# An encoder's tiles moved by 384 bytes: the weights' parts at the operands' place modulo 512

## The chip, the cores and the metric

The kernel runs on one core of a Trainium2 chip. The metric is the device time of one execution in microseconds (us); the time before is the median of three runs. The chip is told of only as this case's runs and traces show it.

## The reference

Two layers over 256 tokens of width 2048, all in float32; each layer reads its 262 MB of weights once.

```python
for i in range(DEPTH):                      # DEPTH = 2
    h = rmsnorm(x, g_mix[i])
    z = h @ w_in[i]                         # diff q, k, v | latents | rope key | two gates
    ...                                     # 8 heads of differential attention -> od
    y_diff = od.reshape(b, s, DIFF_WIDTH) @ w_branch_diff[i]
    ...                                     # 8 heads of multi-head latent attention -> om
    y_mla = om.reshape(b, s, MLA_WIDTH) @ w_branch_mla[i]
    merged = jax.nn.sigmoid(ga) * y_diff + jax.nn.sigmoid(gb) * y_mla
    x = x + merged @ w_out[i]
    gu = rmsnorm(x, g_ffn[i]) @ w_gate_up[i]
    gate, up = jnp.split(gu, 2, axis=-1)
    x = x + (jax.nn.silu(gate) * up) @ w_down[i]
    e = p[i] @ w_ple_in[i]
    x = x + jax.nn.sigmoid(rmsnorm(x, g_ple[i]) @ w_ple_gate[i]) * e
return rmsnorm(x, g_final)
```

## The kernel before

Activations are held with the channels on the 128 partitions and the 256 tokens along the free dimension. Every float32 operand of a large product is split into a high part (rounded to the matmul's fp32r type) and a low part (the rest). An operand of a product, `ua[j]` or `ub[j]`, is one tile of 512 columns: 256 of the high part, then 256 of the low part.

`piece` (line 167) fetches up to eight 128x128 blocks of a weight in one transfer of up to 512 KB, issued on the SyncE queue, into one of four buffers `w32`; ScalarE writes the high part `whi` (line 176), VectorE the low part `wlo` (through the helper on line 72); both have three buffers. `emit` (line 196) then issues a pair of matmuls for each block: line 206 holds the block of `whi` as weights and streams all 512 columns of the operand; line 207 holds the block of `wlo` and streams the operand's first 256 columns. Each matmul is preceded by the load of its own 128x128 weights, 512 bytes of each partition. In the profile a matmul stands under PE and its weight load under PEld, with the line of the matmul. A product over 2048 channels is 16 such pairs. ScalarE and VectorE afterwards join the two halves of the result (lines 231 and 72).

The scores of the second attention (line 336, tiles `S<-fb,fa` and `S<-kr,fc` or `S<-kr,ub`) are blocks of twelve matmuls of 256 columns, each with its own weight load; those that apply the probabilities to the values (line 615, `at<-wt,E`) are blocks of six. The first value product (lines 387 to 389, `mmv<-whi,ua`) streams the weights, 512 columns at a time, and holds the operand.

The order on each engine is set when the program is built, by a scheduler with a timeline of its own; the transfers of the weights are issued ahead as far as the four buffers go.

Tiles that live through the whole kernel stand in the order in which they are made. In the built program `ua` and `ub` come first, at a distance of 2048 bytes, and all begin at 128 modulo 512 (bytes within a partition); then `xT`, at 128; then `gcol`, the factors of the norms, 126 columns (504 bytes, which take up 512); then `rc` and the rest, among them the 128x128 tiles `ident` and `ones` and the slots `fa0` to `fa4` at 160, `kr`, `fb`, `fc` and `fa5` to `fa7` at 256. The temporary pools follow. There `w32`, `whi`, `wlo`, `E`, `E1` and `wt` begin at 256. A weight block is 512 bytes wide and an operand's part 1024, so that every block of `whi` and `wlo` begins at 256 and every part of `ua` and `ub` at 128.

Of the kernel before, what the change touches and what calls it, by code (L numbers as in the profile page):

```python
# [12 lines left out]
F32 = mybir.dt.float32  # L13
# [6 lines left out]
P = 128  # L20
# [16 lines left out]
PT = 8  # L37
W_BUFS = 4
WARM = 8
NO_SYNC = mybir.DependencyInfo(mybir.DependencyClass.NoSync, mybir.DependencyReason.DATA)  # L40

TWO_PI = 2.0 * math.pi
# [8 lines left out]
def encoder(ctx, tc, x, p, positions, cols, lams, wq, wk, wv, wcq, wckv, wkr, wga, wgb,  # L51
# [5 lines left out]
    const = pool("const")  # L57
# [10 lines left out]
    def bank(ps=ps_at, tag="at", name="at", shape=(P, 2 * T)):  # L68
        return ps.tile(list(shape), F32, tag=tag, name=name)
# [22 lines left out]


    xT = const.tile([P, NC, T], F32, name="xT")
    gcol = const.tile([P, cols.shape[1]], F32, name="gcol")
    rc = const.tile([P, rope_c.shape[1]], F32, name="rc")
    nc.scalar.dma_start(gcol, cols)
    off = {}
# [301 lines left out]
    warm = bank()  # L400
    for _ in range(WARM):
        PE.matmul(warm[:, :P], ones, ones, start=True, stop=True)
# [8 lines left out]
    for L in range(DEPTH):  # L411
# [120 lines left out]
        def sigmoid(sg):  # L532
            si = A.activation(sg, sg, AF.Sigmoid)
            tc.add_manual_dep(si.ins, last_exp[0].ins.name, NO_SYNC, reason="one change of tables")

# [248 lines left out]
```

## Time and profile before

| | us |
|---|---|
| median of three runs (2933.39 to 2934.36) | 2933.75 |
| the profiled execution's own time | 2934.72 |
| its span in the trace | 2932.9 |
| PE busy | 2914.7 |
| PEld (weight loads) busy | 2550.8 |
| DVE busy | 2063.6 |
| ACT busy | 1524.5 |

The profiled execution is 0.97 us longer than the median, and its span 1.8 us shorter than its own time. A busy PE says that some matmul was under way at every moment, not that the array took a column at every clock: matmuls overlap, and their ends are modelled. How fast a stage goes is therefore read from the starts of successive matmuls, or from their number in a window of time.

### The profile page before, as it was taken

The page shows a single profiled execution, that of the slowest core. Times are in us where ns is not written, and L with a number is a line of the kernel's source. Part 1 is how long each engine was busy: PE and PEld are TensorE (multiplying, and loading weights), DVE is VectorE, ACT ScalarE, POOL GpSimd, SP SyncE. Part 2 cuts the span into 40 slices and gives each one's busy share as a digit, 9 for nine tenths or more (in the row PEclk, how much of TensorE's full clock was granted, in tenths as well). Part 3 has the DMA queues.
Part 4 walks back from the last instruction along what each step waited for, and adds up shares of the span by engine and source line. Part 5 has one row for each costly group of instructions (what it writes and reads, how often), then busy time and mean ns, then how long its engine had stood idle before and what let it go on. Part 6 is the DMA issues. An engine that isn't in the chain of part 4 may idle for free.

```text
span 2932.9 us, 43979 instructions
## 1 busy us (share of the span) xinstructions
PE 2914.7 (99%) x16750; PEld 2550.8 (87%) x16750; DVE 2063.6 (70%) x3529; ACT 1524.5 (52%) x2529; POOL 1.6 (0%) x8
## 2 busy tenths in 40 slices
PE   9999999999999999999999999999999999999998
PEld 7888888888888888888888888888888888888887
DVE  7897658776666666666859975687666666666676
ACT  6676545544444444445646755455444444444454
POOL 0000000000000000000000000000000000000000
PEclk9999999999999999999999999999999999999999
DMA  6444455555565565555554444555555655655654
GB/s 229 166 161 148 158 188 191 187 186 187 183 193 188 178 191 195 187 187 186 187 186 165 150 153 164 189 190 186 187 187 182 192 188 181 194 188 188 188 185 140
DMA packets 156019, 532.40 MB, mean 182 GB/s; under 512 B 16928, under 2 KB 23840, under 8 KB 155808
## 3 DMA queue, kind: packets, MB, share of 16 engines
q1 hardware_dynamic: 155376, 529.01, 54.5%
q8 instruction: 131, 2.15, 0.3%
q14 instruction: 80, 0.66, 0.1%
q10 hardware_dynamic: 432, 0.59, 0.1%
HBM read 527.43 MB, written 2.10 MB: 181 GB/s over the span
## 4 chain that ended last, share of the span: by engine, by line
PE 99%; DVE 1%; DMA 0%; ACT 0%; SPq 0%; issue 0%; DVEq 0%
PE mm L206 61%; PE mm L207 31%; PE S L336 1%; PE mmv L389 1%; PE mmv L387 1%; PE mmv L388 1%; PE at L354 0%; PE at L558 0%; PE at L615 0%; DMA w<-in_wv 0%; PE at L275 0%; DVE xT L72 0%; PE at L266 0%; DVE wlo L72 0%; DVE a L72 0%; PE at L573 0%
## 5 line engine op out<-in xcount | busy, mean ns | idle before, releaser
L72 DVE TENSOR_TENSOR wlo<-w,whi 128x1024 fp32r<-128x1024 f32 (+2 forms) x1029 | 1229.3, 1195 | 761.6 <-ACT whi L176 749.3
L176 ACT ACTIVATE whi<-w 128x1024 fp32r<-128x1024 f32 (+2 forms) x1029 | 1066.0, 1036 | 1336.4 <-issue 783.8
L206 PE MATMUL mm<-ub,whi 128*128 128x512 f32 x3952 | 1391.3, 394 | 0.0
L206 PE MATMUL mm<-ua,whi 128*128 128x512 f32 x3744 | 1320.3, 394 | 0.0
L207 PE MATMUL mm<-ub,wlo 128*128 128x256 f32 x3952 | 1117.7, 283 | 0.0
L207 PE MATMUL mm<-ua,wlo 128*128 128x256 f32 x3744 | 1059.5, 283 | 0.0
L206 PEld LDWEIGHTS mm<-ub,whi 128*128 128x128 f32 x3952 | 742.0, 188 | 170.3
L206 PEld LDWEIGHTS mm<-ua,whi 128*128 128x128 f32 x3744 | 702.5, 188 | 158.1
L207 PEld LDWEIGHTS mm<-ub,wlo 128*128 128x128 f32 x3952 | 743.2, 188 | 0.8
L207 PEld LDWEIGHTS mm<-ua,wlo 128*128 128x128 f32 x3744 | 704.1, 188 | 2.0
L72 DVE TENSOR_TENSOR a<-mm,join 128x256 f32<-128x256 f32 x421 | 175.2, 417 | 0.3 <-ACT join L231 0.2
L231 ACT ACTIVATE join<-mm 128x256 f32<-128x256 f32 x453 | 166.8, 369 | 5.4 <-PE mm L207 5.1
L72 DVE TENSOR_TENSOR xT<-xT,mm 128x256 f32<-128x256 f32 x256 | 106.9, 420 | 49.6 <-PE mm L207 45.8
L72 DVE TENSOR_TENSOR a<-a,row 128x256 f32<-128x256 f32 x207 | 87.3, 424 | 6.6 <-ACT row L279 0.8
L387 PE MATMUL mmv<-whi,ua 128*128 128x512 f32 x128 | 51.5, 403 | 2.6 <-ACT whi L176 2.6
L72 DVE TENSOR_TENSOR a<-a 128x256 f32<-128x256 f32 x120 | 50.9, 425 | 4.0
L388 PE MATMUL mmv<-whi,ua 128*128 128x512 f32 x128 | 50.9, 399 | 0.0
L72 DVE TENSOR_TENSOR ua<-a,ua 128x256 fp32r<-128x256 f32 x120 | 50.1, 417 | 1.0 <-ACT ua L239 1.0
L239 ACT ACTIVATE ua<-a 128x256 fp32r<-128x256 f32 x120 | 48.4, 403 | 2.6 <-DVE a L72 2.6
L389 PE MATMUL mmv<-wlo,ua 128*128 128x512 f32 x128 | 47.7, 405 | 0.1
L345 ACT ACTIVATE E<-S,nm 128x256 f32<-128x256 f32 x96 | 44.2, 470 | 5.1 <-DVE nm L78 5.0
L72 DVE TENSOR_TENSOR ssq<-ssq,sq 128x256 f32<-128x256 f32 x97 | 40.5, 418 | 0.5 <-ACT sq L258 0.5
(153 smaller groups left out, 1160.3 us busy)
## 6 DMA issues: line engine op xcount, KB each, us to landing
w<-in_w_gate SPq DMA_DIRECT2D x176, 512.0 KB, 4.5
w<-in_w_up SPq DMA_DIRECT2D x176, 512.0 KB, 4.5
w<-in_w_down SPq DMA_DIRECT2D x128, 512.0 KB, 3.5
w<-in_wga SPq DMA_DIRECT2D x64, 512.0 KB, 3.7
w<-in_wgb SPq DMA_DIRECT2D x64, 512.0 KB, 4.4
w<-in_w_out SPq DMA_DIRECT2D x64, 512.0 KB, 4.5
w<-in_w_pg SPq DMA_DIRECT2D x64, 512.0 KB, 3.7
w<-in_w_down SPq DMA_DIRECT2D x64, 384.0 KB, 3.5
```

The lines of the kernel that those rows point to most:

```text
L72: return V.tensor_tensor(out=o, in0=a, in1=b, op=op)
L176: last_split[:] = A.activation(hi[:, :m], w[:, :m], AF.Copy), tt(lo[:, :m], w[:, :m], hi[:, :m].bitcast(F32), ALU.subtract)
L206: PE.matmul(acc, hi[:, s], u, start=start, stop=False)
L207: PE.matmul(acc[:, T:], lo[:, s], u[:, :T], start=False, stop=stop)
L231: A.activation(t, acc[:, T:], AF.Copy)
L239: return A.activation(hi, src, AF.Copy), tt(lo, src, hi.bitcast(F32), ALU.subtract)
L336: PE.matmul(S[:, b, :], q[:, b * P : (b + 1) * P], k, start=j == 0, stop=j == len(pairs) - 1)
L345: last_exp[0] = A.activation(E[:, b, :], S[:, b, :], AF.Exp, bias=nm[:, b : b + 1], scale=scale, accum_out=sm[:, b : b + 1])
L387: PE.matmul(banks[b], xh, hi[:, s], start=a + j == 0, stop=False)
L388: PE.matmul(banks[b], xl, hi[:, s], start=False, stop=False)
L389: last_mm[:] = [PE.matmul(banks[b], xh, lo[:, s], start=False, stop=a + j == n - 1)]
```

## The change

`gcol` is allocated 96 float32 columns (384 bytes) wider, and the kernel uses the first 126 of them as before. `gcol` then takes up 896 bytes where it took up 512, and each tile allocated after it lies 384 bytes further on. In the program built from the changed kernel the instructions are the same, in the same order on every engine, and every line number after the new one is higher by one. `ua`, `ub` and `xT` stay where they are, at 128 modulo 512. `w32`, `whi`, `wlo`, `E`, `E1`, `wt`, `fb`, `fc`, `kr` and `fa5` to `fa7` go from 256 to 128; `fa0` to `fa4`, `ident` and `ones` go from 160 to 32. The results' tiles in PSUM don't move.

```diff
@@ -37,6 +37,7 @@
 PT = 8
 W_BUFS = 4
 WARM = 8
+PAD = 96
@@ -92,7 +93,7 @@
     xT = const.tile([P, NC, T], F32, name="xT")
-    gcol = const.tile([P, cols.shape[1]], F32, name="gcol")
+    gcol = const.tile([P, cols.shape[1] + PAD], F32, name="gcol")[:, : cols.shape[1]]
     rc = const.tile([P, rope_c.shape[1]], F32, name="rc")
```

## The prediction

> **What bounds the kernel now.** I read the page first: busy times, granted clock, the chain that ended last, the costliest groups.
>
> ```profile
> PE 2914.7 (99%) x16750; PEld 2550.8 (87%) x16750; DVE 2063.6 (70%) x3529; ACT 1524.5 (52%) x2529; POOL 1.6 (0%) x8
> ...
> PEclk9999999999999999999999999999999999999999
> ...
> PE 99%; DVE 1%; DMA 0%; ACT 0%; SPq 0%; issue 0%; DVEq 0%
> ...
> L206 PE MATMUL mm<-ub,whi 128*128 128x512 f32 x3952 | 1391.3, 394 | 0.0
> L206 PE MATMUL mm<-ua,whi 128*128 128x512 f32 x3744 | 1320.3, 394 | 0.0
> L207 PE MATMUL mm<-ub,wlo 128*128 128x256 f32 x3952 | 1117.7, 283 | 0.0
> L207 PE MATMUL mm<-ua,wlo 128*128 128x256 f32 x3744 | 1059.5, 283 | 0.0
> ```
>
> TensorE is the bound everywhere: 99% of the chain, idle for nobody before the matmuls of the pairs, at the full clock. There are 3952 + 3744 = 7696 pairs of lines 206 and 207. So the question is not who waits, but how long a pair takes and whether the place of its weights in a partition has a part in it. For that I asked the number of line 206's matmuls in two long windows, and then the timeline of PE alone inside one of them (start, length).
>
> ```profile
> core 0: us, PE busy (x) PEld busy (x), PEclk, DMA share, GB/s
> 500.00:1300.00 800.00, 798.97 (x2277) 427.12 (x2277) 1.00 0.57 187
> 2000.00:2800.00 800.00, 799.05 (x2278) 427.21 (x2277) 1.00 0.58 187
> ```
>
> ```profile
> 700.58 0.40 PE L206 MATMUL mm<-ub,whi 128*128 128x512 f32 x1
> 700.82 0.28 PE L207 MATMUL mm<-ub,wlo 128*128 128x256 f32 x1
> 700.93 0.39 PE L206 MATMUL mm<-ub,whi 128*128 128x512 f32 x1
> 701.16 0.28 PE L207 MATMUL mm<-ub,wlo 128*128 128x256 f32 x1
> 701.28 0.40 PE L206 MATMUL mm<-ub,whi 128*128 128x512 f32 x1
> 701.51 0.28 PE L207 MATMUL mm<-ub,wlo 128*128 128x256 f32 x1
> 701.63 0.40 PE L206 MATMUL mm<-ub,whi 128*128 128x512 f32 x1
> 701.87 0.28 PE L207 MATMUL mm<-ub,wlo 128*128 128x256 f32 x1
> 701.99 0.39 PE L206 MATMUL mm<-ub,whi 128*128 128x512 f32 x1
> ```
>
> A pair takes 800 / 2277 = 351.3 ns, in two windows 1500 us apart. 7696 x 351.3 ns is 2704 us, 92% of the span. Inside it line 207 lasts 0.11 to 0.12 us from its start to the next start, and line 206 the rest, 0.23 to 0.24. The lengths of line 206 come round in threes, short, long, long (0.39, 0.40, 0.40, 0.39), while ScalarE, VectorE and the transfers come and go beside them. So the pair keeps a rhythm of its own, which nothing outside TensorE disturbs.
>
> What would it take without any gap? At the start of the kernel a few matmuls run at half the clock, and there the array itself is the limit:
>
> ```profile
> 12.70:14.80 2.10, 2.10 (x6) 0.50 1.03 403
> ```
>
> ```profile
> 13.12 0.63 PE L387 MATMUL mmv<-whi,ua 128*128 128x512 f32 x1
> ...
> 14.82 0.63 PE L388 MATMUL mmv<-whi,ua 128*128 128x512 f32 x1
> ```
>
> Four starts lie between, so 512 columns take 1.70 / 4 = 0.425 us at clock 0.50, which makes 212.5 ns at the full clock and 106.25 ns for 256 columns: 318.75 ns for a pair. The gap is 351.3 - 318.75 = 32.5 ns a pair, 250 us in the whole kernel. Of it line 207 has about 13 ns (0.12 us against 106) and line 206 about 19. This gap is all that the change can touch.
>
> **The change part by part.** *The instructions.* None is added, removed or moved: the order on every engine is the same, and the bytes of every transfer are. The edit costs nothing by itself, and it does what it says: in the built program `ua` and `ub` stay at 128 modulo 512 and every block of `whi` and `wlo` goes from 256 to 128. What is left are addresses.
>
> *The transfers and the other engines.* The rows of the weights now begin 128 bytes off their old place in `w32`, and nearly all of VectorE's and ScalarE's operands move too.
>
> ```profile
> w<-in_w_gate SPq DMA_DIRECT2D x176, 512.0 KB, 4.5
> ```
>
> ```profile
> ACT whi L176 <- DMA w<-in_wv: 1.7, 2, 1.2
> ```
>
> ```profile
> L72 DVE TENSOR_TENSOR fb<-a,row 128x256 f32<-128x256 f32 x44 | 18.7, 425 | 1.4
> L72 DVE TENSOR_TENSOR fa<-a,row 128x256 f32<-128x256 f32 x32 | 13.4, 419 | 0.3
> ```
>
> A load lands 4.5 us after its issue; four buffers of eight pairs each cover 4 x 8 x 351 ns = 11.2 us, and ScalarE waited for a weight's transfer for 1.7 us in the whole run. A load would have to become twice as slow before it showed. VectorE's adds with results at two different places (`fb` at 256, `fa` mostly at 160) differ by 6 of 425 ns, and VectorE is 1% of the chain, 29 us, of which that is 0.4 us: I take zero, with 0.4 us to either side. Their cover is TensorE's own length; if the pair gets shorter by a few nanoseconds, VectorE at 70% still follows.
>
> *The pair.* Here the trace of before shows no pair with both operands at the same place, so its price has to be bounded. The nearest rows are the score blocks of the second attention's heads 5 to 7, where the streamed operand (`fb`, `kr`) and the weights (`fa5` to `fa7`, `fc`) all lie at 256. In head 4 of the same code `fa4` lies at 160. First the starts in head 7, then the groups in head 7's window, then those in head 4's, then those in a block of line 615, where both also lie at 256:
>
> ```profile
> 329.44 0.52 PE L336 MATMUL S<-kr,fc 128*128 128x256 f32 x3
> 329.80 0.52 PE L336 MATMUL S<-fb,fa 128*128 128x256 f32 x3
> 330.16 0.52 PE L336 MATMUL S<-kr,fc 128*128 128x256 f32 x3
> ```
>
> ```profile
> L336 PEld LDWEIGHTS S<-kr,fc 128*128 128x128 f32 x6 | 0.9, 192 | 0.0
> L336 PEld LDWEIGHTS S<-fb,fa 128*128 128x128 f32 x6 | 0.9, 190 | 0.0
> ```
>
> ```profile
> L336 PEld LDWEIGHTS S<-fb,fa 128*128 128x128 f32 x6 | 0.9, 189 | 0.0
> L336 PEld LDWEIGHTS S<-kr,fc 128*128 128x128 f32 x6 | 0.9, 188 | 0.0
> ```
>
> ```profile
> L615 PEld LDWEIGHTS at<-wt,E 128*128 128x128 f32 x6 | 0.8, 188 | 0.0
> ```
>
> With both at the same place, matmuls of 256 columns follow each other at (330.16 - 329.44) / 6 = 0.120 us: a gap of 120 - 106.25 = 13.75 ns, the same each time, with no rhythm of three. That is what line 207 has already. The open value is line 206's. If a matmul at the same place pays 13.75 ns whatever its length, since it has one weight load beside it either way, line 206 falls to 212.5 + 13.75 = 226.25 ns and the pair to 346.25. I take this value, because it is the gap of the only blocks with both operands at one place that settle into a steady step. The sum is (351.3 - 346.25) x 7696 = 38.9 us less: 2934.72 - 38.9 = 2895.8 us against the profiled execution, and 2895 against the median, which is 0.97 us shorter.
>
> The ends: below, line 206 is always its short form. The query of line 206 gives its lengths as least, median and most:
>
> ```profile
> L206 PE MATMUL mm<-ua,whi x3744: 386/396/583, 55.5 to 2825.9; 128*128 128x512 f32 x198
> ```
>
> The mean is 394 (above), so short throughout is worth 8 ns a pair, 61.6 us: 2872. Long throughout costs 2 to 3 ns, 2 x 7696 = 15 us or a little more, which lies inside what the rivals span. Above, the gap of an aligned matmul could grow with the columns that it streams: 2 x 13.75 = 27.5 ns for line 206, a pair of 212.5 + 27.5 + 120 = 360 ns, 8.7 x 7696 = 67 us more: 3001. The aligned rows lie nearer to 346 than to 360, since each matmul of either length has one load of 512 bytes beside it; but they are all of 256 columns, and that is the weak place of my sum.
>
> **The rivals.** *No effect of the place.* The pair's rhythm would be a matter of TensorE's own clock and queue, and the time would stay at 2933.75. For it: line 615 has both operands at one place too, and its loads take 188 ns as everywhere; and engines that read and write at all places beside TensorE don't touch the rhythm. Against it: in heads 5 to 7 the loads of the same line take 192 instead of 188. The Trainium skill, "SBUF — State Buffer", section "Who interferes with whom", has TensorE read its streamed operand and its weights through two independent ports, and knows contention only on a port pair that VectorE and GpSimd share; by that rule this rival is the outcome. The trace agrees as far as the other engines go; the 192 ns speak against it, though weakly, since head 4 also enters its block in another phase.
>
> *Slower by longer weight loads.* With both at one place the load of a block takes 192 ns instead of 188, as in head 7's rows. Line 206's next weights are loaded while line 207 streams, and line 207 lasts 0.12 us against a load of 0.19, so that the load, not the stream, may set the step. Then each pair is 4 ns longer from the point on where line 207's step follows its load: 4 x 7696 = 30.8 us, 2965. For it: the 192 ns, and that line 207 is already the tighter of the two. Against it: in the very block that has the 192 ns the step is 120 ns, no more than line 207 has now.
>
> *Slower by a gap that grows with the stream*: 3001, worked out above. For it: line 206 has the larger gap already, 19 against 13 ns. Against it: 512 columns are streamed beside one load, as 256 are.
>
> *Faster by the short form alone*: 2872, as above, if the long form is a collision that the new place never has.
>
> **How the numbers follow.** The gap of 13.75 on both lines: 0.33. Short throughout: 0.14. No effect: 0.16. Longer loads: 0.27. A gap that grows: 0.10. Two parts of it are on the faster side, 0.47; the slower side has 0.37. The rows are few and argue for both, so that the likeliest case leads by little. The forecast is 2895. The range of 8 in 10 takes in both faster cases, no effect and the longer loads, and ends between these and the last case, which is left out: 2872 to 2980. The faster cases have a range of their own, 2872 to 2928. About 0.2% (5.9 us, 0.76 ns a pair) is what a measurement of this kernel can tell from no change; the rest of 0.16 around no effect holds what is smaller.
>
> **What would show it.** Everything is in the two windows of 800 us, with line 206 now line 207. At 346.25 ns a pair they hold 2310 matmuls of it instead of 2277; short throughout (343.3 ns) 2330; longer loads (355.3) 2252; a gap that grows (360) 2222; no effect 2277. The lengths of that line should lose their two forms, and the mean length of its loads says whether 188 became 192. In the new numbers, if line 208's step leaves 0.12 us, what failed is that the aligned score blocks stand for the pair's shorter matmul; if only line 207's step differs from 226 ns, it is that the gap doesn't depend on the length. Transfers that hold back ScalarE for more than the 1.7 us of now would show that the cover of 11.2 us didn't do. The forecast is wrong as a whole if the windows hold 2277 or fewer.

## The result, and the profile after

| | before | after |
|---|---|---|
| median, us | 2933.92 (2932.95 to 2935.49, 6 runs) | 2919.62 (2916.80 to 2921.81, 6 runs) |
| profiled execution, its span, us | 2934.72, 2932.9 | 2916.8, 2915.0 |

The changed kernel is faster by 14.3 us: the ratio is 0.9951, with a 95% interval of 0.9938 to 0.9964. The direction is the forecast's, the size is little more than a third of it (38.9 us). The page after, in the lines that answer to those of before:

```profile
PE 2896.3 (99%) x16750; PEld 2527.2 (87%) x16750; DVE 2063.6 (71%) x3529; ACT 1524.1 (52%) x2529; POOL 1.6 (0%) x8
...
PE 99%; DVE 1%; DMA 0%; ACT 0%; SPq 0%; issue 0%; DVEq 0%
...
L207 PE MATMUL mm<-ub,whi 128*128 128x512 f32 x3952 | 1381.0, 395 | 0.0
L207 PE MATMUL mm<-ua,whi 128*128 128x512 f32 x3744 | 1315.7, 396 | 0.0
L208 PE MATMUL mm<-ub,wlo 128*128 128x256 f32 x3952 | 1101.5, 279 | 0.0
L208 PE MATMUL mm<-ua,wlo 128*128 128x256 f32 x3744 | 1046.0, 280 | 0.0
L207 PEld LDWEIGHTS mm<-ub,whi 128*128 128x128 f32 x3952 | 740.8, 188 | 172.3
L208 PEld LDWEIGHTS mm<-ub,wlo 128*128 128x128 f32 x3952 | 744.3, 188 | 0.8
...
w<-in_w_gate SPq DMA_DIRECT2D x176, 512.0 KB, 4.6
```

TensorE is still the bound, and VectorE and ScalarE are as busy as before, to 0.4 us. Note that the mean of one record of line 207 went up, from 394 to 395 and 396 ns, in a kernel that became faster, and that of line 208 went down, from 283 to 279 and 280. The ends are modelled, so a mean record is not a step. The windows of the forecast, with the number of line 207's matmuls in parentheses:

```profile
core 0: us, PE busy (x) PEld busy (x), PEclk, DMA share, GB/s
500.00:1300.00 800.00, 798.99 (x2304) 431.07 (x2303) 1.00 0.59 190
2000.00:2800.00 800.00, 799.06 (x2302) 431.02 (x2301) 1.00 0.59 189
```

27 and 24 pairs more than before at some 347 ns each are 17.7 us, and the two spans differ by 17.9. So the windows hold as much as the whole gain, and the other 1315 us of the span have none on balance. Narrower windows show why. First line 206 of before, then line 207 of after:

```profile
360.00:530.00 170.00, 170.00 (x485) 90.90 (x484) 1.00 0.56 189
800.00:1270.00 470.00, 470.00 (x1339) 251.34 (x1339) 1.00 0.58 188
1290.00:1360.00 70.00, 69.92 (x201) 37.43 (x200) 1.00 0.61 187
1390.00:1450.00 60.00, 60.00 (x172) 32.08 (x172) 1.00 0.54 185
```

```profile
360.00:530.00 170.00, 170.00 (x483) 90.44 (x482) 1.00 0.55 188
800.00:1270.00 470.00, 470.00 (x1357) 254.25 (x1356) 1.00 0.59 191
1290.00:1360.00 70.00, 70.00 (x199) 37.25 (x199) 1.00 0.61 188
1390.00:1450.00 60.00, 60.00 (x171) 31.94 (x170) 1.00 0.57 187
```

In the long feed-forward stage 18 pairs more fit in; in the second gate and the branch products behind it (360 to 530), in the last part of the down product (1290 to 1360) and in the last gate (1390 to 1450), one or two fewer. Differences of one or two counts say little, so here are starts from PE's timeline of after, in a stretch that lost and in one that gained (start, length):

```profile
399.60 0.40 PE L207 MATMUL mm<-ua,whi 128*128 128x512 f32 x1
399.84 0.28 PE L208 MATMUL mm<-ua,wlo 128*128 128x256 f32 x1
399.96 0.40 PE L207 MATMUL mm<-ua,whi 128*128 128x512 f32 x1
...
401.72 0.40 PE L207 MATMUL mm<-ua,whi 128*128 128x512 f32 x1
```

```profile
700.19 0.39 PE L207 MATMUL mm<-ub,whi 128*128 128x512 f32 x1
700.42 0.28 PE L208 MATMUL mm<-ub,wlo 128*128 128x256 f32 x1
700.54 0.39 PE L207 MATMUL mm<-ub,whi 128*128 128x512 f32 x1
...
702.27 0.39 PE L207 MATMUL mm<-ub,whi 128*128 128x512 f32 x1
```

Both fences span six pairs: 2.12 us in the first, 353 ns a pair; 2.08 in the second, 347. Over whole stretches, from the nanosecond starts in the trace, the pair takes 353.33 ns in the one and 346.67 in the other, and hardly anything between; before, it takes 351.1 in every long stretch. The kernel after has **two rhythms**, a quick one 4.4 ns better than before and a slow one 2.2 ns worse. A long stretch keeps the one it has, across the ends of products, for more than 1400 pairs. In layer 1 the long slow stretches are 349 to 535 us, 1282 to 1368 and 1380 to 1452, and layer 2 has them at the same stages. In the long stretches some 1470 us run quickly and some 700 slowly: 4.4 / 351 x 1470 - 2.2 / 351 x 700 = 14 us.

That this equals the difference of the medians is a coincidence. The profiled execution is the fastest of after's six, and its span is 17.9 us shorter than before's. Since the order on TensorE is the same in both, their nanosecond starts can be subtracted matmul by matmul: the pairs' steps give 15.0 of the 17.9 us, and the value products 3.5 (384 steps that are some 5.5 ns shorter are 2.1 of it, the rest is less waiting between them); everything else is 0.6 us longer.

The same starts say which matmul of the pair gained. The table has the mean time from its start to the next start, in ns:

| stretch, us | 512 columns | 256 columns | pair |
|---|---|---|---|
| before, 800 to 1270 | 230.7 | 120.5 | 351.1 |
| after, quick, 640 to 770 | 230.0 | 116.7 | 346.7 |
| after, quick, 800 to 1270 | 231.7 | 115.0 | 346.7 |
| after, slow, 360 to 530 | 236.4 | 116.9 | 353.3 |

The matmul of 256 columns has a shorter step in both rhythms. That of 512 columns stays about where it was in the quick rhythm and is 6 ns longer in the slow one. Over the whole kernel the steps of the former are 33.0 us less, and those of the latter 18.0 us more.

### The profile page after: what moved, and what is told of

It is laid out like the page before. It is cut to its first block, busy times and chain, and to the rows that moved or that the text cites. A ratio compares the mean times of both kernels' runs of the same rounds, so it can differ in the third digit from the quotient of the medians.

```text
span 2915.0 us, 43979 instructions
## 1 busy us (share of the span) xinstructions
PE 2896.3 (99%) x16750; PEld 2527.2 (87%) x16750; DVE 2063.6 (71%) x3529; ACT 1524.1 (52%) x2529; POOL 1.6 (0%) x8
## 4 chain that ended last, share of the span: by engine, by line
PE 99%; DVE 1%; DMA 0%; ACT 0%; SPq 0%; issue 0%; DVEq 0%
PE mm L207 61%; PE mm L208 31%; PE S L337 1%; PE mmv L390 1%; PE mmv L388 1%; PE mmv L389 1%; PE at L355 0%; PE at L559 0%; PE at L616 0%; DMA w<-in_wv 0%; PE at L276 0%; DVE xT L73 0%; PE at L267 0%; DVE wlo L73 0%; DVE a L73 0%; PE at L574 0%
## 5 line engine op out<-in xcount | busy, mean ns | idle before, releaser
L208 PE MATMUL mm<-ub,wlo 128*128 128x256 f32 x3952 | 1101.5, 279 | 0.0
L208 PE MATMUL mm<-ua,wlo 128*128 128x256 f32 x3744 | 1046.0, 280 | 0.0
```

The costliest lines, as they stand in the source:

```text
L208: PE.matmul(acc[:, T:], lo[:, s], u[:, :T], start=False, stop=stop)
```

## The experiments

Each was timed beside the kernel before on the same chip; medians in us, ratios with their 95% interval. The first question was whether the change acts by the *difference of the two operands' places*, and modulo what, or by where things lie at all, or by nothing of the kind.

**Another width of the pad.** Here `PAD` alone is changed. 128 puts the weights at 256 modulo 512 again, as before, though all tiles move as far as in the change.

```diff
-PAD = 96
+PAD = 128
```

> The pad is 512 bytes instead of 384: every tile behind it moves, and all stand where they stood before modulo 512. Theory R (the difference between the weights' and the operand's place modulo 512 sets the pair's rhythm): 2934 us within 2, 351.1 ns a pair in the windows of 800 us (2277 or 2278 pairs). Theory A (the absolute place modulo 512 of the weights): the same. Theory L (a lottery: any move of tiles starts the matmuls in another phase): any time between 2915 and 2935.

2933.83 against 2934.04, ratio 1.0001 (0.9991 to 1.0010). Widening the tile does nothing by itself.

**The same difference elsewhere.** An unused tile of 384 bytes stands ahead of `ua`, and the pad is 0: operands at 0, weights at 128.

```diff
-PAD = 96
+PAD = 0
...
+    const.tile([P, 96], F32, name="ahead")
     ua = [const.tile(
```

> An unused tile of 384 bytes ahead of the operands, and no pad in the norms' factors: the weights' parts go to 128 modulo 512 as in the change, but the operands go from 128 to 0, so that the difference stays at 128 bytes. Theory R: 2934 us within 2. Theory A: 2920 us, as with the change. Theory L: anything between 2915 and 2935.

2933.9, ratio 0.9999 (0.9989 to 1.0008). Weights that begin at 128 are not what helps.

**A quarter and a half of the way.** `PAD = 32` puts the weights at 384, 256 away from the operands; `PAD = 64` at 0, 384 away.

> The pad is 128 bytes: the weights' parts stand at 384 modulo 512, 256 behind the operands. Theory R: a rhythm of its own, neither 351.1 nor 346.7/353.3 ns a pair needs to come back; time away from 2934 by more than 2 us either way. Theory L: 2915 to 2935 with the rhythms that are known. If only the weights' being at the same place matters, 2934 us.

> The pad is 256 bytes: the weights' parts stand at 0 modulo 512, 384 behind the operands. Theory R: a rhythm of its own; the value products at the start had this difference in the kernel before (streamed weights at 256, held operand at 128), with no steady step and 232 ns for 512 columns, so 2930 to 2945 us. If only the weights' being at the same place matters, 2934 us.

`PAD = 32` takes 2917.29, ratio 0.9943 (0.9928 to 0.9958); `PAD = 64` takes 2934.42, ratio 1.0001 (0.9991 to 1.0010). The same windows of the second gate and the feed-forward, first with 32, then with 64:

```profile
360.00:530.00 170.00, 170.00 (x482) 90.38 (x481) 1.00 0.59 188
800.00:1270.00 470.00, 470.00 (x1357) 254.17 (x1357) 1.00 0.62 191
```

```profile
360.00:530.00 170.00, 170.00 (x486) 90.96 (x485) 1.00 0.57 189
800.00:1270.00 470.00, 470.00 (x1340) 251.42 (x1339) 1.00 0.61 188
```

With 32 the counts are those of after, with 64 those of before. So it is the difference modulo 256 bytes that decides: 0 or 256 apart gives the two rhythms, and even the same stretches are slow; 128 or 384 apart gives 351.1 ns. The "modulo 512" of the change's description is twice too strict.

**Smaller steps.** `PAD = 16` makes the difference 192, `PAD = 112` makes it 64.

> The pad is 64 bytes: the weights' parts stand at 320 modulo 512, 192 behind the operands (192 modulo 256). If only the difference modulo 256 counts and 128 is simply the difference that isn't 0: 2934 us. If the pair's rhythm varies with each difference: another rhythm, 2910 to 2960 us.

> The pad is 448 bytes: the weights' parts stand at 192 modulo 512, 64 behind the operands. If only the difference modulo 256 counts and 128 is simply the difference that isn't 0: 2934 us. If the rhythm varies with each difference: another rhythm, 2910 to 2960 us; if it is modulo 128 that a part of it depends on, the same as the run with 192.

2935.84, ratio 1.0004 (0.9995 to 1.0014), and 2948.8, ratio 1.0049 (1.0034 to 1.0064). With 64 every long stretch takes 353.3 ns a pair, in the one form of 235 and 118 ns (after's slow rhythm has 241, 236 and 232 for the 512 columns in turn); with 192 there are stretches of 353.3 and others of 348.9 ns, so that its median near before's is that of a mixture. PE's timeline with 64:

```profile
899.64 0.40 PE L207 MATMUL mm<-ub,whi 128*128 128x512 f32 x1
...
902.11 0.40 PE L207 MATMUL mm<-ub,whi 128*128 128x512 f32 x1
```

Seven pairs lie in these 2.47 us, 353 ns each. Among the places tried the time goes from 2917 to 2949 us, and before's was not a bad one.

**One part at a time.** An unused tile of 128 bytes before `wlo` leaves only `whi` at the operands' place (`PAD = 96`), one of 384 bytes moves only `wlo` there (`PAD = 0`).

```diff
+        wts.tile([P, 32], F32, tag="gap", name="gap", bufs=1)   # 96 in the second
         lo = wts.tile(
```

> Only the high parts stand at the operands' place; an unused tile of 128 bytes puts the low parts back to 256 modulo 512. The load of a high part lies beside the stream of 256 columns, that of a low part beside the stream of 512. If each load's own difference sets the gap of the matmul beside it: line 208's step as in the change (116 ns), line 207's as before (231 ns): 347 ns a pair, 2900 us. If both are needed for the two rhythms: 351 ns, 2934 us.

> Only the low parts stand at the operands' place, by an unused tile of 384 bytes ahead of them; the high parts stay at 256 modulo 512. If each load's own difference sets the gap of the matmul beside it: the step of 512 columns as in the change (233 ns), that of 256 as before (120.5 ns): 353.5 ns, 2952 us. If both are needed for the two rhythms: 351 ns, 2934 us.

`whi` alone: 2925.65, ratio 0.9969 (0.9958 to 0.9981), a pair of 350.0 ns. `wlo` alone: 2940.6, ratio 1.0021 (1.0011 to 1.0030), 352. The kernel before took 2934.35 beside both. The expected 2900 and 2952 us, by which each load's own place would set the gap of the matmul beside it, both fail, as does the 2934 of the other case. The effects don't add up (-8.7 and +6.3 us alone, -14.3 together): the step of a matmul depends on its neighbour's place too.

**Runs of one length.** The forecast's 13.75 ns came from blocks of matmuls of one length. Here each piece issues its eight `whi` matmuls first and then its eight `wlo` ones, once with the pad and once without.

```diff
-                PE.matmul(acc[:, T:], lo[:, s], u[:, :T], start=False, stop=stop)
+
+        for j, u in enumerate(() if whole else us):
+            s, stop = slice((at + j) * P, (at + j + 1) * P), last and j == len(us) - 1
+            PE.matmul(acc[:, T:], lo[:, s], u[:, :T], start=False, stop=stop)
```

> The change's places, and another order in each piece of up to eight blocks: first all matmuls of the high parts (512 columns), then all of the low parts (256). Theory M (at the same place modulo 256 a run of matmuls of one length settles at 16 cycles of 1.2 GHz over its stream, 226.7 and 120.0 ns; the trouble is the alternation of two lengths, which has a quick rhythm of 346.7 ns a pair and a slow one of 353.3): 346.7 ns a pair in every stage, 4.4 ns x 7696 = 34 us below before, 2900 us. Theory E (the rhythm is drawn at the entry of each stage and the order inside has no part): 2917 to 2920 us, with both rhythms in the windows.

> The kernel before with that same order. Theory M: at a difference of 128 the runs of one length don't settle; the value products' 232 ns for 512 columns and the last product's 118.5 ns for 256 make 350.5 to 351 ns a pair, so 2930 to 2935 us. If the order alone is what helps: 2900 us here too.

With the pad 2917.22, ratio 0.9938 (0.9924 to 0.9953); without it 2934.8, ratio 1.0000 (0.9990 to 1.0009). The mean steps (360 to 530 us) are 230.0 and 119.1 ns with the pad, 232.7 and 118.6 without. With the pad a run of 256 columns stands at 120 ns from its third step on (114, 119, 120, 120 ...), while one of 512 comes to 226 or 227 only in its last three (233, 236, 228, 233, 231, 226, 227, 227). So 2900 us is missed, and the order gains nothing over the change. For 256 columns in runs of one length, the same place is no gain at all: 119.1 against 118.6. The long runs themselves are in the value products, 512 columns each; PE's timeline of after:

```profile
18.63 0.39 PE L388 MATMUL mmv<-whi,ua 128*128 128x512 f32 x1
18.86 0.39 PE L389 MATMUL mmv<-whi,ua 128*128 128x512 f32 x1
...
20.67 0.39 PE L389 MATMUL mmv<-whi,ua 128*128 128x512 f32 x1
```

Nine steps in 2.04 us are 227 ns (about 232.5 before, from the nanosecond starts). This is the forecast's 226.25 for 512 columns, but in a run of 512 alone, which no pair is.

**What picks the rhythm.** The quick stretch that begins at 537 us follows a place where the scheduler lets two matmuls of line 207 meet and then two of line 208; at the like exchange at 1281 us the rhythm turns slow. One theory was that such an exchange turns the one rhythm into the other. The next kernel makes one in an early product of four stages: the second of the attentions' second gate, of the output and of the last part of the down product, the fourth of the last gate.

```diff
                 PE.matmul(acc, hi[:, s], u, start=start, stop=False)
+                if swap and j == 0:
+                    continue
+                if swap and j == 1:
+                    PE.matmul(acc[:, T:], lo[:, at * P : (at + 1) * P], us[0][:, :T], start=False, stop=False)
                 PE.matmul(acc[:, T:], lo[:, s], u[:, :T], start=False, stop=stop)
```

> The change, and in four places of each layer one extra exchange of two matmuls (high, high, low, low instead of high, low, high, low) in the second or fourth product of a stage: second gate, output projection, last part of the down projection, last gate. In the change's trace such an exchange, which the scheduler makes at a few seams by itself, turned the slow rhythm (353.3 ns a pair) into the quick one and the quick into the slow. Theory T (the places allow two rhythms, and an exchange turns one into the other): nearly all pairs at 346.7 ns, so about a third of the pairs gain 6.7 ns: 2917 to 2920 less 15, 2900 to 2906 us. Theory P (the rhythm belongs to the stage: its products, pools or transfers): the same stages stay slow, 2917 to 2921 us.

2912.91, ratio 0.9925 (0.9908 to 0.9941), between the two times that were expected. Layer 1's second gate with the branch products, then the last down part and the last gate:

```profile
360.00:530.00 170.00, 170.00 (x491) 91.94 (x491) 1.00 0.60 191
...
1290.00:1360.00 70.00, 70.00 (x199) 37.25 (x199) 1.00 0.63 188
1390.00:1450.00 60.00, 60.00 (x174) 32.44 (x173) 1.00 0.61 193
```

The first window runs quickly now, 491 for 483, though nothing in its stages but one exchange, ahead of it, is different: the rhythm is no property of the stage, its data or its transfers. But the theory is only half right. Of the eight added exchanges three met a quick rhythm (the output of layer 1, the last down part of both layers), and all three turned it slow. Five met a slow one: three turned it quick (layer 1's second gate and both last gates), two didn't (layer 2's second gate and output). And the scheduler's own exchange at 782 us, which turned quick into slow in after until the next irregular place 4 us later, left the rhythm quick here. The next kernel has that order, high, high, low, low, throughout.

```diff
-                PE.matmul(acc[:, T:], lo[:, s], u[:, :T], start=False, stop=stop)
+                if j % 2 == 0 and j + 1 < len(us):
+                    continue
+                for i in range(j - j % 2, j + 1):
+                    PE.matmul(acc[:, T:], lo[:, (at + i) * P : (at + i + 1) * P], us[i][:, :T], start=False, stop=stop and i == j)
```

> The change's places, and the exchange everywhere: two matmuls of 512 columns, then two of 256, and so on. If the alternation of two lengths is what brings rhythms other than 16 cycles a matmul: still a mixture, 346 to 352 ns a pair, 2900 to 2935 us. If each exchange costs nothing and settles: 346.7 ns, 2900 us.

2913.42, ratio 0.9928 (0.9913 to 0.9942). It has one rhythm, 348.4 ns a pair, in every long stretch: four groups of two pairs between these starts, 2.79 us / 8.

```profile
899.92 0.63 PE L207 MATMUL mm<-ub,whi 128*128 128x512 f32 x2
...
902.71 0.40 PE L207 MATMUL mm<-ub,whi 128*128 128x512 f32 x1
```

**A break that always enters the quick rhythm.** In the kernels with after's order, a stretch that began after the norm's small matmuls against `ones` (one column, float32) was quick, as at 1370 us of after, where the pairs before them were slow. The exception is two places (99 and 1544 us of after) where the norm's other float32 matmul, of 256 columns, stands directly ahead of them; that one alone begins the slow stretch of the last gate (1379 us). So two matmuls of one column, whose results nobody uses, follow the first piece of one product in each stage that is slow in after (the second of the second gate, the third of the last down part, the fifth of the last gate) and in the output's third product, because the scheduler's exchange in the output's second product would meet a quick rhythm now. The second kernel has the same breaks with `PAD = 0`.

```diff
             emit(acc, hi, lo, 0, us[a : a + m], a == 0, a + m == n, whole)
+            if nudge and a == 0:
+                with tc.issue_after(last_pair[0].ins):
+                    idle = bank()
+                    for b in range(2):
+                        PE.matmul(idle[:, b : b + 1], ones, ones[:, 0:1], start=b == 0, stop=b == 1)
```

> The change, and in four places of each layer two extra float32 matmuls of one column (their result is not used), just behind the scheduler's own seams: second gate, output projection, last part of the down projection, last gate. Theory N (the event at the entry decides, and this one always leaves the quick rhythm): the 1968 pairs of the long slow stretches go from 353.3 to 346.7 ns, 13 us, less some 0.5 us for each of eight breaks: 2909 to 2911 us, with 346.7 ns a pair in all long stretches. Theory P (the rhythm belongs to the stage): 353.3 ns stays where it is, 2923 to 2925 us.

> The kernel before with the same breaks. At a difference of 128 every stretch had 351.1 ns a pair whatever went ahead: 2934 us and about 4 us for the breaks, 2938 us. If a break by itself makes pairs quicker: below 2934 us.

With the pad 2909.04 (2908.27 to 2909.89), ratio 0.9914 (0.9899 to 0.9929): the fastest of all, 26.1 us below before on the same chip. With the breaks alone 2937.98, ratio 1.0012 (1.0002 to 1.0021), so they cost some 3 us of their own, and on equal breaks the pad is worth 28.9. The four windows with pad and breaks:

```profile
360.00:530.00 170.00, 170.00 (x492) 92.00 (x491) 1.00 0.60 191
800.00:1270.00 470.00, 470.00 (x1357) 254.19 (x1356) 1.00 0.62 191
1290.00:1360.00 70.00, 70.00 (x203) 37.85 (x203) 1.00 0.63 190
1390.00:1450.00 60.00, 60.00 (x174) 32.47 (x174) 1.00 0.61 188
```

Where after had 483, 199 and 171 there are 492, 203 and 174, and in the stage that was quick already the same 1357. All eight breaks lead into the quick rhythm. What decides is how a stretch is entered.

## Where the prediction was right, and where it failed

*The bound.* Right: TensorE stays the bound, no other engine's busy time moved by more than 0.4 us, and the steps of TensorE's matmuls account for the change of the time. But the sum counted the pairs alone. The value products, whose streamed weights also come to the place of the held operand, have no term in it, and no reason for that is given; in the profiled executions they are 3.5 of the 17.9 us.

*The transfers and the other engines at nothing.* Right: a load of `in_w_gate` lands after 4.6 us where it took 4.5, VectorE's sum is the same, and ScalarE's waits for a weight's transfer in this row, 3.8 us where it had 1.7, stay without effect:

```profile
ACT whi L177 <- DMA w<-in_wv: 3.8, 3, 1.9
```

*The pair at 346.25 ns: 226.25 for line 206 and an unchanged 120 for line 207.* This is the step that failed, and in two ways.

The first is the two terms. The text held that line 207 has the gap of an aligned matmul already and that line 206 alone would gain. The runs show the opposite: in the quick rhythm the 512 columns step at 230.0 to 231.7 ns (230.7 before), and it is the 256 columns that go from 120.5 to 116.7 or 115.0. Both terms are some 3 to 5 ns off, in opposite directions, so that their sum of 346.67 comes within half a nanosecond of 346.25 by luck. The text had given signs for this, in the new line numbers. Line 208's step leaves 0.12 us, by 3 to 5 ns, so the aligned score blocks don't stand for the pair's shorter matmul; line 207's step differs from 226 ns too, so they don't stand for the longer one either. The 227 and 120 ns do occur, but in runs of one length.

The second is "settles": one gap was to hold everywhere. The same place allows a second rhythm, 353.33 ns a pair, slower than before's, which keeps itself up and holds about a third of the time of the long stretches. All pairs at 346.67 would save 4.4 ns x 7696 = 34 us; after's pairs have 15.0 of it in the profiled execution. With the entries of four stages mended the whole kernel is 26 us below before, with breaks that cost 3.

The rows that gave the price show the weakness themselves. In after, the score blocks of heads 5 to 7 still have both operands at one place (128 now), and they no longer step evenly: 121, 120, 124, 118, 117, 121 ns, twice over. The starts of three matmuls each in head 7 are 0.37, 0.35 and 0.37 us apart, where they were 0.36 each time:

```profile
326.66 0.53 PE L337 MATMUL S<-fb,fa 128*128 128x256 f32 x3
327.03 0.52 PE L337 MATMUL S<-kr,fc 128*128 128x256 f32 x3
327.38 0.52 PE L337 MATMUL S<-fb,fa 128*128 128x256 f32 x3
327.75 0.52 PE L337 MATMUL S<-kr,fc 128*128 128x256 f32 x3
```

The blocks that apply the probabilities, with both operands at one place before and after, did the reverse in heads 5 to 7: they had 116 to 121 ns before and stand at 120 from their second step in after. So a steady 120 ns was no property of the place. The text called the blocks' 256 columns "the weak place of my sum"; weaker was that they are blocks of one length, and that the dozen's even step was taken for a rule.

*"The lengths should lose their two forms."* Half right: some quick stretches have a single form, while after's stretches at 353.33 keep a beat of three.

*The windows.* They were to hold 2310 and hold 2304 and 2302, close to the forecast while the time is not. By chance nearly all of their 1600 us lies on stretches at 346.67, and most of the stretches at 353.33 lie outside. A window confirms a step only for its own stages, and a count of pairs says nothing of the two steps inside a pair.

*The rivals.* No effect of the place: wrong, though a move that leaves the difference at 128 or makes it 384 has indeed none. By the Trainium skill, "SBUF — State Buffer", section "Who interferes with whom", the streamed operand and the weights come through two independent read ports. If that means that the place of the one can't matter to the other, the runs disagree, since the time moves from 2917 to 2949 us when the pad alone, and with it the difference of the two places, changes. They don't show whether a port, a bank or something else does it.

Longer weight loads: wrong, the loads of the pairs stay at 188 ns, in slow stretches too (the rows of the windows give 90.44 us / 482 there and 254.25 / 1356 in the quick one, 188 both). The 192 ns of head 7 don't come with the place, since the same load has 188 in after:

```profile
L337 PEld LDWEIGHTS S<-kr,fc 128*128 128x128 f32 x6 | 0.9, 188 | 0.0
```

A gap that grows with the columns: its 360 ns a pair are not reached. In the pair the gap of 512 columns is indeed the larger one, 17.5 to 19 ns in the quick rhythm and 24 in the slow against 9 to 11 for 256 columns, but in runs of one length the two are nearly equal (227 - 212.5 = 14.5 against 13.75). The short form alone (343.3): not reached, as quick stretches stay at 346.67.

## What to carry to other kernels

Where TensorE is the bound and each fp32r matmul loads its own weights, the places of weights and streamed operand are worth a try modulo 256 bytes, and a difference that is only half way may be worse than the one there was: here 64 apart costs 15 us and 0 apart brings 14. Read such a step from starts in every stage, not from mean records or from one window, for the same code can run in two rhythms in one execution. A price taken from a uniform run isn't the price in an alternation, and a sum that fits is no proof of its terms: measure each step by itself. Where a stretch may lock into either of two rhythms, try an interruption at its beginning, with the same interruption on the kernel before as the control.

## What the runs showed of the hardware that was not expected

- The step of a pair of fp32r matmuls (512 and 256 columns, each with its own load of 128x128 weights) follows the difference of the operands' places: 346.67 or 353.33 ns at 0 and 256 bytes, 351.1 at 128 and 384, 353.3 at 64, 348.9 or 353.3 at 192. Only these differences were tried.
- Who gains depends on the order. From 128 to 0 bytes apart, in the alternation of two lengths, the 256 columns gain (120.5 to 115.0 or 116.7 ns) and the 512 don't (230.7 to 230.0 or more). In runs of one length the 512 gain (232.5 to 227) and the 256 don't (118.6 to 119.1, in runs of eight).
- Rhythms keep themselves up. One exchange of two matmuls or two one-column matmuls change the pair's step by 2% for hundreds of pairs after it (some 510 each after the exchange in layer 1's second gate and after the break there).
- After's six runs spread over 5.0 us and before's over 2.5; with a difference of 192, which also has two rhythms, ten runs spread over 9.5, and with 64, which has one, four over 1.7. That some executions enter a stretch differently would explain it, but only the profiled executions show their stretches, so this is not shown.
- Why two rhythms exist at 0 and 256, and why a break by one-column matmuls leads to the quick one while an exchange may lead to either, stays open: the trace shows starts, and nothing of what TensorE waits for between them.
